# Making the weights' low part with an adding DMA instead of a VectorE subtraction

## The chip, the cores and the metric

The kernel runs on one core of a Trainium2 chip. The metric is the device time of one execution in microseconds; lower is better. The median of three runs before the change is 1457.76 us (1455.7 to 1457.97).

## What is computed

Two layers of a streaming encoder over 640 tokens: 512 frames of one new stream and 16 frames of each of eight running streams. A layer is

```python
proj = rms_norm(x, norm1) @ w_in                       # (640, 1024) @ (1024, 1536)
mix  = concat(rg_lru(proj), s5(proj), attention(proj)) # 256 + 256 + 512 columns
x = x + mix @ w_out                                    # (1024, 1024)
act = square(relu(rms_norm(x, norm2) @ w_up))          # (1024, 4096)
x = x + act @ w_down                                   # (4096, 1024)
```

with one more RMSNorm at the end. Everything is float32, and most of the arithmetic is in the four weight matrices of each layer.

## The kernel before

**Layout.** The 640 tokens are two groups of 320 (256 frames of the prompt and 64 of the samples), `g` = 0 and 1. Activations stand transposed, channels on the 128 partitions, tokens along the free dimension.

**Split products.** The matmuls take `float32r` operands, and each operand is held as a high part in that type and the rest. A unit of weights is 1024 x 128, loaded as two halves of 128 x 4 x 128 (256 KB): `raw` by SyncE's queue (`wload`, issue at L229 through `dma`). `wunit` (L237 to L246) makes two tiles of each half: `wh` (the high part, ScalarE, L243) and `wl` (the low part, raw minus high, VectorE, L244). `product` (L248 to L255) then runs, for each of eight blocks of 128 rows, three matmuls of 320 columns into one PSUM bank: high by high (L252), high by low of the activations (L253), low by high (L254). A half therefore feeds 12 matmuls for one group of tokens.

**Buffers.** `raw`, `wh` and `wl` each have four buffers, so weights are made up to four halves ahead of their use. A buffer of `raw` comes free when both `wh` and `wl` have been made from it; buffers of `wh` and `wl` when the product has read them.

**Stages.** `in_proj` (12 units per layer and group), the mixers (`lru`, `s5`, `attention`; small matmuls with much work on VectorE, ScalarE and GpSimd), `out_proj` (8 units), and `mlp` in four quarters of 8 units of `w_up` and 8 of `w_down`. The second and third quarter run both groups on each unit (`mlp(L, 1, (0, 1), ...)`), so a half feeds 24 matmuls there; everywhere else it feeds 12. In all 544 halves are loaded and split: 192 + 192 + 96 + 64 of w_up, w_down, w_in and w_out. `out_proj` and the last quarter also run the next norm's parts for each finished tile: L268 and L281 on ScalarE, L269 on VectorE, L288 on GpSimd.

**Order.** The program is written stage by stage; a scheduler that simulates time fixes the order of the instructions on each engine, and places the work of one stage's mixers between the products of others. Every engine then takes its own list in order. GpSimd's list before holds no DMA.

Of the kernel before, what the change touches and what calls it, by code (L numbers as in the profile page):

```python
# [11 lines left out]
F32 = mybir.dt.float32  # L12
F32R = mybir.dt.float32r
I32 = mybir.dt.int32
AF = mybir.ActivationFunctionType
# [35 lines left out]
def _cols(a):  # L51
    """(..., 128 r) vectors as columns."""
    a = np.asarray(a)
    return a.reshape(-1, 128).T
# [5 lines left out]
def _layout(inputs):  # L60
    """The arrays in the order in which the chip reads them: moves of elements only."""
# [6 lines left out]
    def tiles(w):  # L68
        # (1024, 128 n) -> (n, 128 p, 8 k, 128)
        return w.reshape(8, 128, -1, 128).transpose(2, 1, 0, 3)  # L70
# [9 lines left out]
    # small vectors, one column each  # L80
# [13 lines left out]
    # S5 input and output matrices: halves (re, im) and (im, re) on the partitions  # L94
# [53 lines left out]
def encoder_kernel(ctx: ExitStack, tc: tile.TileContext, a, o):  # L148
# [35 lines left out]
    # ------------------------------------------------------------ constants  # L184
# [4 lines left out]
    # the table of the exponentials comes in before the first load has landed  # L189
# [41 lines left out]
    # ------------------------------------------------------------ weights  # L231
# [5 lines left out]
    def wunit(src, raws=None):  # L237
        out = []
        for n in range(2):
            raw = raws[n] if raws else wload(src, n)  # L240
            h = wp.tile([128, 4, 128], F32R, tag="wh", name="wh")
            l = wp.tile([128, 4, 128], F32R, tag="wl", name="wl", bufs=4)
            act(h, raw, AF.Copy)  # L243
            tt(l, raw, h.bitcast(F32), OP.subtract)  # L244
            out.append((h, l))
        return out  # L246
# [10 lines left out]
    # ------------------------------------------------------------ norms  # L257
    class Norm:
# [41 lines left out]
        def rsqrt(self):  # L300
            """8/3 / sqrt(mean + eps) with the tokens on the partitions (0-127, 128-255, 192-319)."""
# [5 lines left out]
            # a first guess from the exponent, one step of second order and one of third  # L307
# [23 lines left out]
    # ------------------------------------------------------------ small vectors  # L331
# [6 lines left out]
    # ------------------------------------------------------------ accurate exp on small tiles  # L338
    def exp_small(out, x, n):
        """out = exp(x) on [128, n], to about one unit in the last place."""  # L340
# [16 lines left out]
    # ------------------------------------------------------------ LRU constants  # L357
# [24 lines left out]
    # ------------------------------------------------------------ S5 constants  # L382
# [49 lines left out]
    def cmul(eng, out, jout, wr, wis, z, jz, tmp, conj=False):  # L432
        """out = w z (stacked halves), jout = its halves swapped; wis has the half's sign."""
        A, B = (OP.subtract, OP.add) if conj else (OP.add, OP.subtract)
        eng.tensor_tensor(tmp, wis, jz, OP.mult)
        eng.tensor_tensor(out, wr, z, OP.mult)
        eng.tensor_tensor(out, out, tmp, A)
        if jout is not None:
            eng.tensor_tensor(tmp, wis, z, OP.mult)
            eng.tensor_tensor(jout, wr, jz, OP.mult)  # L440
            eng.tensor_tensor(jout, jout, tmp, B)

    def s5_const(L):
# [10 lines left out]
        # input matrices: slot s of a pair of groups is abar^(3-s) Bbar  # L454
# [15 lines left out]
        # output matrices  # L470
# [9 lines left out]
        # causal products inside a block: those with the block's last output, then the rows moved up  # L480
# [9 lines left out]
        # rotation tables by doubling  # L490
# [37 lines left out]
    # ------------------------------------------------------------ per layer small tensors  # L528
# [12 lines left out]
    # ------------------------------------------------------------ input projection  # L541
    def gelu2(eng, out, x):
        """out = 2 gelu(x)"""
# [97 lines left out]
    # ------------------------------------------------------------ RG-LRU  # L641
    def lru(L, P, g, q, mix, c):
# [10 lines left out]
        for ct in range(2):  # L653
# [4 lines left out]
            # the newest rows before the convolution  # L658
# [7 lines left out]
            # decay a = exp(-2 w) and 1 - a^2 = tanh(w) (1 + a)^2  # L666
# [7 lines left out]
        # injection of the running states into the column before each sample  # L674
# [18 lines left out]
    # ------------------------------------------------------------ S5  # L693
    def s5(L, P, g, q, mix, c):
        K = P["S5"]
        u = q.ub
        # zz takes the place of U
# [5 lines left out]
        # inputs by blocks: rows (group of the pair, t, channel)  # L703
# [41 lines left out]
        # outputs  # L745
# [18 lines left out]
        # states after the last block  # L764
# [22 lines left out]
    # ------------------------------------------------------------ attention  # L787
    def attention(L, P, g, q, mix, c):
        # the samples' scratch
        kcT, p = c.at(0, 2, 2, 144), [c.at(640 + 288 * n, 2, 144) for n in range(2)]  # L790
        vc, pt = c.at(1280, 2, 2, 128), [c.at(640 + 288 * n, 2, 128) for n in range(2)]
        # those of the second pair of samples start at partition 32
        half = [slice(32 * n, 32 * n + 16) for n in range(2)]
        vn, pn = ([c.at(o, 2, 128)[h] for h in half] for o in (1792, 2048))
        # the prompt's, in the same place: keys' windows of 192 columns with 64 zeros on each side
# [18 lines left out]
        def soft(b, x, sk, nsk, one):  # L814
            """Exponentials of the scores in b over their sum with the sink's."""
# [116 lines left out]
    # ------------------------------------------------------------ output projection and MLP  # L932
# [39 lines left out]
    # ------------------------------------------------------------ the program  # L972
# [14 lines left out]
    # the tensor engine's clock rises while the first loads are under way  # L987
# [31 lines left out]
    # ------------------------------------------------------------ final norm  # L1019
# [36 lines left out]
```

## Time and profile before

| what | value |
|---|---|
| runs | 1455.7, 1457.76, 1457.97 us (median 1457.76) |
| profiled execution, from its first to its last instruction | 1454.2 us |
| median of the runs over that span | 3.6 us more |
| TensorE, matmuls | 1404.7 us busy, 97% |
| VectorE | 924.5 us, 64% |
| ScalarE | 662.4 us, 46% |
| GpSimd | 377.0 us, 26% |
| DMA from HBM | 151.02 MB read, mean of all traffic 107 GB/s |
| mean granted TensorE clock | 0.979 of 2.4 GHz |

A group of instructions is one line of the kernel on one engine; "idle before" is the time that the engine stood still right before such instructions, and what ended it. Matmuls are pipelined, so the 314 ns of one overlap with the next: the step from one to the next is about 0.147 us. Where an engine is not the one that ends a stretch, its idle time costs nothing.

### The profile page before, as it was taken

To read this page: it belongs to the slowest core of one execution; us is meant where nothing else is said; L and a number is where in the kernel's file an instruction comes from. 1 tells how busy PE (TensorE), PEld (TensorE's weight loads), DVE (VectorE), ACT (ScalarE), POOL (GpSimd) and SP (SyncE) were. 2 spreads that over 40 slices of the span, in tenths; PEclk is the share of its full clock that TensorE was granted. 3 is DMA by queue.
4 is the path that set the end of the run, shared out by engine and by line. 5 is a ranking of instruction groups with operands and counts; after the bars stand their busy time and mean duration, and the time that the engine had idled before them with its cause. 6 is when DMAs were issued, how large, how long until landed. Compare 5 with 4: busy or idle time off the path is not lost.

```text
span 1454.2 us, 25829 instructions
## 1 busy us (share of the span) xinstructions
PE 1404.7 (97%) x9540; PEld 1336.3 (92%) x9540; DVE 924.5 (64%) x1858; ACT 662.4 (46%) x1387; POOL 377.0 (26%) x565
## 2 busy tenths in 40 slices
PE   7699999999999999999999999999999999999997
PEld 7688688899999999999987898789999999999997
DVE  8999889856544344357687768875664434434564
ACT  6566565545422122135674667453543312313543
POOL 3847269401010011072244225320110100100111
PEclk9999899999999999999998999899999999999998
DMA  6232122344422222234422342224443222223452
GB/s 244 86 109 81 50 95 97 105 150 140 152 80 78 76 80 73 73 107 157 140 91 73 120 137 92 68 95 145 149 146 106 73 73 73 80 78 104 153 174 94
DMA packets 91389, 156.27 MB, mean 107 GB/s; under 512 B 14336, under 2 KB 18304, under 8 KB 91264
## 3 DMA queue, kind: packets, MB, share of 16 engines
q1 hardware_dynamic: 91264, 154.63, 32.0%
q8 instruction: 75, 1.23, 0.4%
q14 instruction: 50, 0.41, 0.1%
HBM read 151.02 MB, written 3.37 MB: 106 GB/s over the span
## 4 chain that ended last, share of the span: by engine, by line
PE 80%; DVE 11%; POOL 4%; issue 3%; ACT 2%; DMA 1%; SPq 0%; DVEq 0%; POOLq 0%
PE mm L254 24%; PE mm L252 24%; PE mm L253 24%; DVE wl L244 2%; PE att L899 1%; PE att L878 1%; PE s L755 1%; PE s L753 1%; PE att L176 1%; PE s L176 1%; PE fin L326 0%; PE att L663 0%; PE s L721 0%; PE s L779 0%; DVE bigr L269 0%
## 5 line engine op out<-in xcount | busy, mean ns | idle before, releaser
L254 PE MATMUL mm<-bigr,wl 128*128 128x320 f32 x2688 | 840.9, 314 | 22.6 <-DVE wl L244 22.6
L252 PE MATMUL mm<-bigr,wh 128*128 128x320 f32 x2688 | 840.2, 313 | 1.7 <-ACT wh L243 1.1
L253 PE MATMUL mm<-bigr,wh 128*128 128x320 f32 x2688 | 839.1, 313 | 1.0 <-DVE bigr L269 1.0
L243 ACT ACTIVATE wh<-raw 128x512 fp32r<-128x512 f32 x544 | 340.7, 630 | 494.4 <-PE mm L253 469.9
L254 PEld LDWEIGHTS mm<-bigr,wl 128*128 128x128 f32 x2688 | 509.8, 190 | 34.7 <-DVE wl L244 27.4
L252 PEld LDWEIGHTS mm<-bigr,wh 128*128 128x128 f32 x2688 | 509.4, 190 | 7.9 <-issue 5.0
L253 PEld LDWEIGHTS mm<-bigr,wh 128*128 128x128 f32 x2688 | 509.5, 190 | 6.9 <-issue 3.9
L244 DVE TENSOR_TENSOR wl<-raw,wh 128x512 fp32r<-128x512 f32 x544 | 399.7, 736 | 179.6 <-ACT wh L243 158.9
L156 POOL TENSOR_SCALAR bigr<-t 128x320 fp32r<-128x320 f32 x128 | 63.0, 493 | 566.3 <-ACT t L952 566.3
L934 DVE TENSOR_TENSOR xT<-xT,mm 128x320 f32<-128x320 f32 x160 | 77.7, 486 | 127.5 <-PE mm L254 127.4
L952 ACT ACTIVATE t<-t 128x320 f32<-128x320 f32 x128 | 59.9, 470 | 137.9 <-DVE t L951 132.3
L954 DVE TENSOR_TENSOR bigr<-t,bigr 128x320 fp32r<-128x320 f32 x128 | 69.7, 546 | 69.6 <-POOL bigr L156 69.3
L951 DVE SCALAR_TENSOR_TENSOR t<-mm,r 128x320 f32<-128x320 f32 x124 | 60.6, 488 | 81.5 <-PE mm L254 81.4
L288 POOL TENSOR_TENSOR ss<-ss,sq 128x320 f32<-128x320 f32 x58 | 56.9, 981 | 195.7 <-ACT sq L281 185.6
L833 POOL TENSOR_SCALAR att<-att,st 128x192 f32<-128x192 f32 (+3 forms) x40 | 37.2, 931 | 79.5 <-DVE st L831 43.6
L824 ACT ACTIVATE att<-att,st 128x192 f32<-128x192 f32 (+3 forms) x80 | 30.7, 389 | 28.3 <-DVE st L822 22.1
L269 DVE SCALAR_TENSOR_TENSOR bigr<-xT,sm,bigr 128x320 fp32r<-128x320 f32 x64 | 39.7, 629 | 3.8 <-ACT bigr L268 3.6
L268 ACT ACTIVATE bigr<-xT,sm 128x320 fp32r<-128x320 f32 x64 | 34.4, 558 | 11.1 <-DVE xT L934 7.8
L281 ACT ACTIVATE sq<-xT 128x320 f32<-128x320 f32 x66 | 30.4, 460 | 9.9 <-DVE xT L934 3.7
L878 PE MATMUL att<-kT,q 64*64 64x192 f32 (+2 forms) x256 | 28.1, 329 | 2.5 <-ACT att L824 2.1
L605 POOL TENSOR_TENSOR sw<-sw,cs 128x320 f32<-128x320 f32 x20 | 19.4, 969 | 33.6 <-ACT sw L604 28.3
L176 PE MATMUL att<-ident,att 128*128 128x128 f32 (+1 forms) x144 | 24.6, 280 | 3.2 <-DVE att L833 1.0
(287 smaller groups left out, 1078.6 us busy)
## 6 DMA issues: line engine op xcount, KB each, us to landing
raw<-w_up SPq DMA_DIRECT2D x192, 256.0 KB, 2.6
raw<-w_down SPq DMA_DIRECT2D x192, 256.0 KB, 2.6
raw<-w_in SPq DMA_DIRECT2D x96, 256.0 KB, 2.6
raw<-w_out SPq DMA_DIRECT2D x64, 256.0 KB, 2.5
xT<-x SPq DMA_DIRECT2D x8, 320.0 KB, 5.7
yT<-xT SPq DMA_DIRECT2D x8, 320.0 KB, 2.5
cs<-rope SPq DMA_DIRECT2D x4, 320.0 KB, 4.4
gg<-gg SPq DMA_DIRECT2D x2, 512.0 KB, 5.1
```

The lines of the kernel that those rows point to most:

```text
L156: return G.tensor_scalar(out, in_, 1.0, 0.0, OP.mult, OP.add)
L176: PE.transpose(out, in_, ident[0:n, 0:n])
L243: act(h, raw, AF.Copy)
L244: tt(l, raw, h.bitcast(F32), OP.subtract)
L252: mm(pt, lhsT=h[:, k % 4], rhs=m[:, k, 0], start=k == 0, stop=False)
L253: mm(pt, lhsT=h[:, k % 4], rhs=m[:, k, 1], start=False, stop=False)
L254: mm(pt, lhsT=l[:, k % 4], rhs=m[:, k, 0], start=False, stop=k == 7)
L288: G.tensor_tensor(self.ss, self.ss, sq, OP.add)
L934: tt(xT[:, g, k], xT[:, g, k], pt, OP.add)
L951: V.scalar_tensor_tensor(t, pt, 0.0, norm.r, OP.max, OP.mult)
L952: act(t, t, AF.Square)
L954: tt(am[:, f, 1], t, am[:, f, 0].bitcast(F32), OP.subtract)
```

## The change

The low part is no longer raw minus high on VectorE. ScalarE writes the negative of the high part into `wl`, and a DMA issued from GpSimd's queue adds `raw` to it in place (`wl += raw`). The high part, the loads, the matmuls and the number of buffers stay. The diff's other lines delete comments and texts; they do nothing. After L244 all line numbers are one higher.

```diff
@@ -241,7 +241,8 @@
             h = wp.tile([128, 4, 128], F32R, tag="wh", name="wh")
             l = wp.tile([128, 4, 128], F32R, tag="wl", name="wl", bufs=4)
             act(h, raw, AF.Copy)
-            tt(l, raw, h.bitcast(F32), OP.subtract)
+            act(l, h.bitcast(F32), AF.Copy, scale=-1.0)
+            G.dma_start(l, raw, accum_op=OP.add)
             out.append((h, l))
         return out
```

A buffer of `raw` now comes free when the adding DMA has landed, and so does `wl` become ready.

The scheduler places the new instructions. ScalarE's list in the first output projection (`out_proj`, layer 0, group 0) before the change; `wh` from `raw` is a high part, `bigr` and `sq` are the next norm's parts (L268, L281):

```order
L243 ACTIVATE wh_3748<-raw_3746 128x512
L243 ACTIVATE wh_3754<-raw_3752 128x512
L268 ACTIVATE bigr_3574<-xT_85,sm_86 128x320
L281 ACTIVATE sq_3700<-xT_85 128x320
L243 ACTIVATE wh_3791<-raw_3789 128x512
L243 ACTIVATE wh_3797<-raw_3795 128x512
L268 ACTIVATE bigr_3574<-xT_85,sm_86 128x320
L281 ACTIVATE sq_3743<-xT_85 128x320
```

The same place after the change (L269 and L282 are the former L268 and L281, L244 is the negative of the high part):

```order
L243 ACTIVATE wh_3814<-raw_3812 128x512
L269 ACTIVATE bigr_3670<-xT_85,sm_86 128x320
L282 ACTIVATE sq_3757<-xT_85 128x320
L244 ACTIVATE wl_3815<-wh_3814 128x512
L243 ACTIVATE wh_3852<-raw_3850 128x512
L244 ACTIVATE wl_3853<-wh_3852 128x512
L243 ACTIVATE wh_3859<-raw_3857 128x512
L269 ACTIVATE bigr_3670<-xT_85,sm_86 128x320
L282 ACTIVATE sq_3802<-xT_85 128x320
L244 ACTIVATE wl_3860<-wh_3859 128x512
```

Of the two halves of a unit, one has the norm's two instructions between its high part and its low part now; the other has them next to each other.

GpSimd's list at that place before the change holds the norm's running sums (`ss`, L288) alone:

```order
L288 TENSOR_TENSOR ss_3575<-ss_3575,sq_3657 128x320
L288 TENSOR_TENSOR ss_3575<-ss_3575,sq_3700 128x320
L288 TENSOR_TENSOR ss_3575<-ss_3575,sq_3743 128x320
L288 TENSOR_TENSOR ss_3575<-ss_3575,sq_3786 128x320
L288 TENSOR_TENSOR ss_3575<-ss_3575,sq_3829 128x320
```

After the change it holds two adds (L245) for each sum (now L289), and parts of the S5 tables (`tab`), which the scheduler has moved here from an earlier place:

```order
L245 DMA wl_3815<-raw_3812 128x512
L518 TENSOR_TENSOR tab_93<-tab_93 128x16x31
L245 DMA wl_3853<-raw_3850 128x512
L506 TENSOR_TENSOR tab_93<-tab_93 128x16
L289 TENSOR_TENSOR ss_3671<-ss_3671,sq_3802 128x320
L245 DMA wl_3860<-raw_3857 128x512
L514 TENSOR_TENSOR tab_93<-tab_93 128x16x31
L515 TENSOR_TENSOR tab_93<-tab_93 128x16x31
L517 TENSOR_TENSOR tab_93<-tab_93 128x16x31
L245 DMA wl_3898<-raw_3895 128x512
```

An add stands behind whatever GpSimd has in front of it, the sum of the last tile among that.

## Rows read from the trace of the kernel before

**Rows 1.** The page: busy time, and the span in 40 slices.
```profile
PE 1404.7 (97%) x9540; PEld 1336.3 (92%) x9540; DVE 924.5 (64%) x1858; ACT 662.4 (46%) x1387; POOL 377.0 (26%) x565
PE   7699999999999999999999999999999999999997
```

**Rows 2.** The page: the chain that ended last, shares of the span by engine and line.
```profile
PE 80%; DVE 11%; POOL 4%; issue 3%; ACT 2%; DMA 1%; SPq 0%; DVEq 0%; POOLq 0%
PE mm L254 24%; PE mm L252 24%; PE mm L253 24%; DVE wl L244 2%; PE att L899 1%; PE att L878 1%; PE s L755 1%; PE s L753 1%; PE att L176 1%; PE s L176 1%; PE fin L326 0%; PE att L663 0%; PE s L721 0%; PE s L779 0%; DVE bigr L269 0%
```

**Rows 3.** Groups by line: busy us, mean ns | idle us before, what ended it.
```profile
L254 PE MATMUL mm<-bigr,wl 128*128 128x320 f32 x2688 | 840.9, 314 | 22.6 <-DVE wl L244 22.6
...
L244 DVE TENSOR_TENSOR wl<-raw,wh 128x512 fp32r<-128x512 f32 x544 | 399.7, 736 | 179.6 <-ACT wh L243 158.9 <-PE mm L253 11.9
L243 ACT ACTIVATE wh<-raw 128x512 fp32r<-128x512 f32 x544 | 340.7, 630 | 494.4 <-PE mm L253 469.9 <-DMA raw<-w_in 8.3 <-PE mm L254 3.9
...
L288 POOL TENSOR_TENSOR ss<-ss,sq 128x320 f32<-128x320 f32 x58 | 56.9, 981 | 195.7 <-ACT sq L281 185.6 <-DVE rsq L310 6.6 <-ACT st L829 3.4
...
L268 ACT ACTIVATE bigr<-xT,sm 128x320 fp32r<-128x320 f32 x64 | 34.4, 558 | 11.1 <-DVE xT L934 7.8 <-DMA xT<-x 2.4
...
L281 ACT ACTIVATE sq<-xT 128x320 f32<-128x320 f32 x66 | 30.4, 460 | 9.9 <-DVE xT L934 3.7 <-POOL ss L288 2.7 <-DVE ss L285 2.2
...
L743 POOL TENSOR_TENSOR bigf<-bigf,tab 128x640 f32<-128x640 f32 x8 | 17.7, 2217 | 5.2 <-ACT bigf L741 5.2
```

**Rows 4.** Stretches, L243 alone: length, ScalarE busy (halves), clock, DMA share, GB/s.
```profile
290.80:399.90 109.10, 37.19 (x59) 1.00 0.45 147
399.90:618.00 218.10, 39.23 (x62) 1.00 0.23 77
618.00:654.40 36.40, 9.95 (x17) 1.00 0.35 107
654.40:727.10 72.70, 24.16 (x40) 1.00 0.45 148
...
836.20:872.50 36.30, 11.12 (x18) 1.00 0.43 137
...
981.60:1090.60 109.00, 38.46 (x61) 1.00 0.44 147
...
1127.00:1308.80 181.80, 32.92 (x52) 1.00 0.23 76
1308.80:1345.10 36.30, 10.06 (x16) 1.00 0.30 104
1345.10:1417.80 72.70, 24.73 (x40) 1.00 0.49 164
```

**Rows 5.** Timelines in the first full-rate stretch: start us, length us, engine, line, what.
```profile
301.56 0.63 ACT L243 ACTIVATE wh<-raw 128x512 fp32r<-128x512 f32 x1 [1.13 <-PE mm L253]
303.32 0.63 ACT L243 ACTIVATE wh<-raw 128x512 fp32r<-128x512 f32 x1 [1.13 <-PE mm L253]
...
302.22 0.69 DVE L244 TENSOR_TENSOR wl<-raw,wh 128x512 fp32r<-128x512 f32 x1 [1.07 <-ACT wh L243]
...
302.94 0.33 SPq L229 DMA_DIRECT2D raw<-w_out  x1
```

**Rows 6.** DMA issues: count, KB each, us to landing; last, raw's landings, 290.8:399.9.
```profile
raw<-w_up SPq DMA_DIRECT2D x192, 256.0 KB, 2.6
...
raw<-w_out SPq DMA_DIRECT2D x64, 256.0 KB, 2.5
...
tab<-bc SPq DMA_DIRECT2D x4, 256.0 KB, 4.5
...
Mm<-Mm SPq DMA_DIRECT2D x4, 24.0 KB, 1.9
...
DMA to landing us min/median/max: 2.5/2.6/3.7
```

**Rows 7.** Two stretches: length, busy us (instructions) of PE, PEld, DVE, ACT, POOL.
```profile
0.00:290.80 290.80, 259.17 (x1724) 224.30 (x1725) 263.36 (x614) 175.73 (x424) 172.41 (x236) 0.95 0.33 108
290.80:399.90 109.10, 109.10 (x741) 107.43 (x740) 64.51 (x116) 50.00 (x88) 9.29 (x14) 1.00 0.45 147
```

**Rows 8.** Chain that ended last, by line: within 0:290.8, then within 727.1:981.6.
```profile
by line: issue 8.6%; DVE wl L244 8.0%; PE mm L254 7.2%; PE mm L252 6.7%; PE mm L253 6.7%; PE s L755 3.1%; PE att L878 3.0%; PE s L753 2.8%; PE att L899 2.5%; PE s L721 2.0%; DVE bigf L657 2.0%; PE att L176 1.8%; DVE bigr L269 1.8%; DMA xT<-
...
by line: PE mm L252 16.6%; PE mm L253 16.4%; PE mm L254 16.2%; issue 4.5%; PE att L878 4.2%; PE att L899 4.0%; DVE wl L244 3.4%; PE s L755 2.6%; PE att L176 2.5%; PE s L753 2.3%; POOL bigf L743 1.9%; PE s L779 1.8%; PE s L176 1.4%; PE att L
```

## The prediction

> **What bounds the kernel now.** I read the page first. TensorE is busy 97% of the span of 1454.2 us, in nearly every slice, VectorE 64%, ScalarE 46%, GpSimd 26% [rows 1]. The chain that ended last says the same: 80% is TensorE, with 72% on lines 252 to 254, the three matmuls of a product; VectorE holds 11%, and the line that this change removes, L244, 2% [rows 2]. The groups show how little TensorE waits for it: 22.6 us in all before the low parts' matmuls, released by L244 [rows 3]. So what can be won is some 20 to 30 us, although 544 instructions of 736 ns (399.7 us) leave VectorE. The question is whether the new way of making a low part is as well hidden as the old one.
>
> For that I cut the span into stretches by how fast weight halves (128x512, one instruction of L243 each) are used [rows 4]. Five stretches run at full rate, 59 + 40 + 18 + 61 + 40 = 218 halves in 109.1 + 72.7 + 36.3 + 109.0 + 72.7 = 399.8 us, 1.83 us each, with the DMA engines busy 0.43 to 0.49. Two stretches (62 and 52 halves, 399.9 us) use each half for both token groups and need one only every 3.5 us. The rest (the first 290.8 us, the mixers of layer 1, changes of stage) uses one in 2 to 3.3 us.
>
> The timeline inside the first full-rate stretch shows the ring [rows 5]. ScalarE writes a high part of 0.63 us every 1.76 us, each time released by L253, that is when TensorE has finished with the buffer of four halves before. VectorE's low part follows 0.03 us later, and 0.03 us after that ends SyncE issues the next load, because the raw buffer is free. A load lands 2.6 us after its issue (at most 3.7 here) [rows 6]. Four buffers make a lap 4 x 1.76 = 7.04 us. Used of it today: 0.63 + 0.03 + 0.69 + 0.03 + 2.6 = 3.98 us. The raw ring has 3.06 us to spare. That spare time is what the change spends.
>
> **The change, part by part.**
>
> *Removed:* L244 on VectorE. In the full-rate stretches VectorE is not the limit (64.5 of 109.1 us busy [rows 7]), so there it gives nothing. In the first 290.8 us VectorE is busy 263.4 us [rows 7] and L244 has 8.0% of the chain, 23 us; in 727 to 982 us 3.4%, 9 us [rows 8]. Upper bound of the gain: 32 us.
>
> *Added on ScalarE:* 544 copies, written as the high part is (128x512, 630 ns [rows 3]): 343 us, of which none is new waiting where ScalarE has room: 50.0 + 59 x 0.63 = 87 of 109.1 us in the first full-rate stretch [rows 7, 4]. One place is tight. During an output projection each product (two halves, 3.52 us) also has L268 and L281, 558 + 460 ns [rows 3]; with 4 x 0.63 that is 3.54 us. There the new order puts those two between a high part and its low part, which adds 1.02 us to every second lap. 64 halves are of that kind (w_out [rows 6]), up to 1.02 / 4 = 0.26 us each: 16 us.
>
> *Added on GpSimd:* 544 issues. The trace has no DMA from this queue. The nearest rows are SyncE's issue of 0.33 us [rows 5] from below, and from above GpSimd's long instructions, 0.98 us (L288) to 2.2 us (L743) [rows 3]. I take 1.0 us, since an engine that has to work a descriptor list out is nearer to a long instruction than to SyncE's. In the full-rate stretches GpSimd is nearly idle (9.3 of 109.1 us) and 59 us more fit. In the first 290.8 us its 172.4 us [rows 7] grow by 88 to 260, so that the bound of that stretch moves from VectorE to GpSimd rather than goes away. I set the two against each other at zero there, with ends of -32 us and +40 us (every other one of 88 issues holding up something for its 1.0 us).
>
> *Added on the DMA engines, and the wait:* a low part is now ready when an add of 256 KB, SBUF to SBUF, has landed. Call A the time from ScalarE's copy to that landing. Two things wait for A: TensorE, and the raw buffer, which the add still reads, so SyncE's next load is behind it. TensorE needs the low part three halves after the high part was begun, 5.28 us plus 0.1 us; the copies take 1.32 us, so A may be 4.1 us. The raw lap is 0.63 + 0.03 + 0.63 + 0.03 + A + 0.03 + 2.6 = 3.95 + A, so there A may be only 3.1 us. The raw ring gives way first.
>
> A from rows: a small copy within SBUF takes 1.9 us from issue to landing, a 256 KB load 2.6 [rows 6], so 256 KB of transfer are 0.7 us. An add has three streams (raw in, low part in, low part out) where a load has two: 1.5 times, 1.05 us. GpSimd's issue is 0.65 us longer than SyncE's. A = 1.9 + 1.05 + 0.65 = 3.6 us, and a lap of 7.55 us gives 1.89 us per half. Bounds: 2.6 us if the add goes like a load from SyncE, and 7 us if issue and transfer behave like the slowest landings of a transfer this size (4.5 us, tab<-bc [rows 6]) with 2.2 us of GpSimd before it.
>
> The 16 DMA engines are a second limit. A half costs them 0.45 x 109.1 / 59 = 0.83 us now [rows 4]. With an add of 1.25 us at 1.5 times it is 2.08 us, above the 1.76 us that TensorE needs. Loads and adds then stand behind one another, half of the other's transfer on average, 0.9 us per lap: (7.55 + 0.9) / 4 = 2.11 us. Both limits say a little over 2.1. I take 2.15 us, since 1.5 is the least that three streams can mean.
>
> *Sum.* Full-rate stretches: 218 x 2.15 - 399.8 = +69 us. Output projections: +16. First stretch and mixers: 0. Stretches at 3.5 us per half: 0, as 2.15 is far below. That makes 1454.2 + 85 = 1539.2 us of span. The median of the runs, 1457.76 us, stands 3.6 us above the profiled span: 1543 us.
>
> **The rivals.**
>
> *Two full reads.* If the read side of the DMA engines is the limit, an add costs twice a load, 0.83 + 1.66 = 2.49 us per half: 218 x 2.49 - 399.8 = +143 us, and about 1601 us. For it: a load's 0.7 us for 256 KB is already near all that the engines do. Against it: no row separates read and write. The Trainium skill (Collectives: The Full Stack, section "The bandwidth ceiling: the fold count and why AG ≠ RS ≠ AR") holds that an add in the DMA path runs at half a copy's rate because it reads two sources; no run here shows it yet, and by it this rival would be the forecast. Chance 0.2.
>
> *Adds much slower still, or GpSimd the gate.* With A = 7 us a half takes (3.95 + 7) / 4 = 2.74 us: 218 x 2.74 - 399.8 = +198, and some +18 where 17 and 16 halves fall into 36 us [rows 4]: about 1673 us. GpSimd works in order, so an add behind an instruction that waits for a mixer gives the same picture. Against it: GpSimd is idle nine tenths of the full-rate stretches. Chance 0.15.
>
> *The ring holds, and VectorE's relief is all that is left.* The point is A = 3.1 us. With the add at 2.6 to 3.1 us from copy to landing and the DMA engines not in each other's way, the full-rate stretches stay at 1.76 us, and of the 32 us on the chain half come back: about 1442 us, faster. For it: 0.5 us is all that separates my 3.6 from it. Against it: the DMA engines would have to do 2.08 us of work in 1.76. Chance 0.11, of which 0.04 that gain and new waits cancel.
>
> *A little over:* A of 3.2 to 3.5 us and little queueing, 1461 to 1500 us, chance 0.1. The forecast itself, 1500 to 1575 us, has the rest, 0.44.
>
> **How the numbers follow.** A measurement of this kernel can tell about 0.2%, 3 us, from no change. Faster 0.07, same 0.04, all other cases slower, 0.89. Below 1465 us lies 0.11, and above 1690 us, past the third case, some 0.08; the range is 1465 to 1690 us.
>
> **What the profile after would show.** Right: VectorE's busy time near 525 us, ScalarE's near 1005; in the full-rate stretches high parts every 2.0 to 2.3 us, with ScalarE's L243 released by the load of raw where it now is by L253; TensorE's idle time before lines 252 and 254; DMA share near or above 0.8 there; adds landing 3.5 to 4.5 us after issue; the 3.5 us stretches as long as before. Wrong: high parts still every 1.76 us (the ring held); or lines 254 waiting for GpSimd's queue with raw long landed (GpSimd is the gate); or the 3.5 us stretches longer, which needs A above 10 us.

## The result

The change makes the kernel slower: 1706.36 us (median of four runs, 1695.44 to 1709.08) against 1457.26 us, a ratio of 1.170 [1.166, 1.174]. The forecast was 1543 us with a range to 1690 us: the direction was right, the loss of 249 us is nearly three times the 85 us that were worked out.

The page of the profile after (a span of 1702.2 us), which answers to [rows 1]: busy time, TensorE's 40 slices, and the two DMA queues (packets, MB, share of the 16 engines' time).

```profile
span 1702.2 us, 27064 instructions
PE 1481.5 (87%) x9540; PEld 1369.2 (80%) x9540; DVE 565.2 (33%) x1314; ACT 966.6 (57%) x1931; POOL 802.0 (47%) x1109
PE   6779989768789999978899888987878999997786
q0 software_dynamic: 78336, 142.64, 48.2%
q1 hardware_dynamic: 91264, 154.63, 28.1%
```

TensorE's row of nines has holes in it now. The second queue, q0, is new: it holds the adds, 142.64 MB (544 of 256 KB), and they take more of the DMA engines than the kernel's whole other traffic on q1. The chain that ended last, to be laid beside [rows 2], shows what filled the holes:

```profile
PE 42%; DMA 31%; ACT 10%; DVE 7%; issue 6%; POOL 2%; SPq 0%; ACTq 0%; POOLq 0%; DVEq 0%
DMA wl<-raw 13%; PE mm L255 13%; PE mm L253 12%; PE mm L254 12%; DMA raw<-w_down 7%; DMA raw<-w_up 5%; ACT wh L243 4%; DMA raw<-w_in 3%; ACT wl L244 3%; DMA raw<-w_out 3%; POOL wl L245 1%; DMA tab<-bc 1%; PE att L879 1%; PE att L900 1%; DVE bigf L740 1%
```

TensorE's share fell from 80% to 42%, and DMA's rose from 1% to 31%: 13% are the adds, wl<-raw, and some 18% the loads of raw. The groups (busy us, mean ns | idle us before, what ended it), beside [rows 3]; L253 to L255 are the former L252 to L254:

```profile
L255 PE MATMUL mm<-bigr,wl 128*128 128x320 f32 x2688 | 868.4, 326 | 132.1 <-DMA wl<-raw 131.4
L253 PE MATMUL mm<-bigr,wh 128*128 128x320 f32 x2688 | 858.0, 320 | 48.5 <-ACT wh L243 46.0 <-issue 2.0 <-DVE t L609 0.2
...
L245 POOL DMA_DIRECT2D wl<-raw x544 | 495.0, 927 | 681.4 <-ACT wl L244 628.3 <-issue 11.5 <-DMA raw<-w_down 9.3
L243 ACT ACTIVATE wh<-raw 128x512 fp32r<-128x512 f32 x544 | 341.4, 628 | 541.8 <-PE mm L254 220.0 <-DMA raw<-w_down 121.6 <-DMA raw<-w_up 97.1
L244 ACT ACTIVATE wl<-wh 128x512 fp32r<-128x512 f32 x544 | 340.7, 628 | 12.6
```

TensorE stands 132.1 us before low parts that have not landed (22.6 us before), and 48.5 us before high parts. L243 used to be released almost by TensorE alone; now some 220 us of its idle time end with a load of raw. That is the raw ring: the load comes late because the add has held its buffer. SyncE's own waits (us in total, times, longest) show it, in the changed kernel and before:

```profile
SPq L229 <- DMA wl<-raw: 1367.6, 524, 11.1
```

```profile
SPq L229 <- DVE wl L244: 965.7, 464, 10.0
```

GpSimd's issue is 0.93 us, and 628 of the 681 us before it end with ScalarE's copy.

**Where the 248 us lie.** Cut by stages (from the first low-part matmul of a stage to that of the next, in both traces), the spans differ as follows:

```
                                         halves   before us   after us   difference
until the first low-part matmul                       7.9       15.7       +7.8
in-projections to up-projection, layer 0   80       272.2      301.3      +29.1
full rate, one group                      224       422.0      597.5     +175.5
both groups on a half, 3.5 us             128       452.2      450.3       -1.9
mixers of layer 1 and what lies in them   112       300.0      337.5      +37.5
```

The full-rate stages went from 1.88 to 2.67 us per half. Windows of four pieces (length, busy us of PE, PEld, DVE, ACT and POOL, granted clock, DMA share, GB/s): the start, a 3.5-us stretch, layer 1's second in-projection, and one full-rate stage of 16 halves.

```profile
0.00:113.50 113.50, 79.34 (x427) 72.79 (x428) 74.94 (x241) 75.08 (x154) 68.93 (x115) 0.80 0.70 175
491.50:716.50 225.00, 225.00 (x1535) 225.00 (x1536) 46.67 (x96) 93.30 (x159) 69.74 (x96) 1.00 0.65 152
968.40:1046.00 77.60, 65.47 (x432) 58.44 (x431) 34.98 (x71) 60.62 (x122) 46.58 (x65) 0.96 0.80 180
1134.00:1175.10 41.10, 31.09 (x192) 28.34 (x193) 4.80 (x10) 20.08 (x34) 15.62 (x19) 1.00 0.92 202
```

In the full-rate stage TensorE is busy for 31.1 of 41.1 us and every other computing engine for half of it or less, the granted clock is 1.00, its upper level, and the DMA engines are 0.92 busy (0.43 to 0.49 before [rows 4]). In the 3.5-us stretch TensorE has no hole, with the same adds under it.

One lap of the ring in that full-rate stage, first from the timeline of ScalarE (start us, length us; in brackets the idle time before, and what ended it):

```profile
1142.05 0.64 ACT L243 ACTIVATE wh<-raw 128x512 fp32r<-128x512 f32 x1 [3.76 <-PE mm L253]
1142.72 0.63 ACT L244 ACTIVATE wl<-wh 128x512 fp32r<-128x512 f32 x1
1144.19 0.63 ACT L243 ACTIVATE wh<-raw 128x512 fp32r<-128x512 f32 x1 [0.84 <-DMA raw<-w_down]
```

then from that of GpSimd:

```profile
1143.65 0.86 POOL L245 DMA_DIRECT2D wl<-raw  x1 [4.17 <-ACT wl L244]
```

The landings in that stage, of the adds (by the tile wl) and of the loads (by their line, L229):

```profile
DMA to landing us min/median/max: 3.5/4.6/6.2
...
DMA to landing us min/median/max: 2.8/3.6/5.1
```

and those of the adds in a 3.5-us stretch, 1468 to 1524 us:

```profile
DMA to landing us min/median/max: 3.2/3.3/3.8
```

ScalarE's copy ends at 1143.35 and GpSimd issues 0.3 us later. Followed through the trace, from one high part to the next one made from the same buffer, the laps that begin in that stage take, in the mean, 0.63 + 0.03 + 0.63 + 0.29 us to the add's issue, 4.75 to its landing, 0.08 to the load's issue, 3.61 to its landing, and 0.25 until ScalarE takes it up: 10.27 us, a fourth of it 2.57 us. The stage took 41.1 / 16 = 2.57. The chain within it agrees, with 79% of it in these two kinds of transfer:

```profile
by line: DMA raw<-w_down 37.2%; DMA wl<-raw 33.1%; issue 10.9%; DMA raw<-w_out 8.8%; ACT wh L243 4.7%; ACT wl L244 4.5%; POOL wl L245 1.3%; ACT t L953 1.1%; POOLq L245 0.2%; SPq L229 0.2%; ACTq L243 0.1%
```

So the ring closes at 2.57 us. But its transfers are slow because they share the engines: where nothing presses, an add lands in 3.3 us, and a load took 2.6 us before [rows 6]. Theory 1 says that the DMA engines are the limit: an add of 0.482 x 1702.2 / 544 = 1.51 us of all 16 and a load of 0.281 x 1702.2 / 544 x 142.6 / 154.6 = 0.81 us (the weights are 142.6 of q1's 154.63 MB) make 2.3 us per half, whatever the buffers. That price is not made by the crowding itself: the 3.5-us stretch above, where TensorE never waits, has 0.65 x 225.0 / 64 = 2.29 us for each of its 64 halves. Theory 2, the rival, says that the four raw buffers are: with more of them the loss would go.

### The profile page after: what moved, and what is told of

Read it like the earlier page. It is cut to its first block, busy times and chain, and to the rows that moved or that the text cites. A ratio compares the mean times of both kernels' runs of the same rounds, so it can differ in the third digit from the quotient of the medians.

```text
span 1702.2 us, 27064 instructions
## 1 busy us (share of the span) xinstructions
PE 1481.5 (87%) x9540; PEld 1369.2 (80%) x9540; DVE 565.2 (33%) x1314; ACT 966.6 (57%) x1931; POOL 802.0 (47%) x1109
## 3 DMA queue, kind: packets, MB, share of 16 engines
q0 software_dynamic: 78336, 142.64, 48.2%
q1 hardware_dynamic: 91264, 154.63, 28.1%
## 4 chain that ended last, share of the span: by engine, by line
PE 42%; DMA 31%; ACT 10%; DVE 7%; issue 6%; POOL 2%; SPq 0%; ACTq 0%; POOLq 0%; DVEq 0%
DMA wl<-raw 13%; PE mm L255 13%; PE mm L253 12%; PE mm L254 12%; DMA raw<-w_down 7%; DMA raw<-w_up 5%; ACT wh L243 4%; DMA raw<-w_in 3%; ACT wl L244 3%; DMA raw<-w_out 3%; POOL wl L245 1%; DMA tab<-bc 1%; PE att L879 1%; PE att L900 1%; DVE bigf L740 1%
## 5 line engine op out<-in xcount | busy, mean ns | idle before, releaser
L255 PE MATMUL mm<-bigr,wl 128*128 128x320 f32 x2688 | 868.4, 326 | 132.1 <-DMA wl<-raw 131.4
L253 PE MATMUL mm<-bigr,wh 128*128 128x320 f32 x2688 | 858.0, 320 | 48.5 <-ACT wh L243 46.0
L254 PE MATMUL mm<-bigr,wh 128*128 128x320 f32 x2688 | 850.0, 317 | 0.0
L245 POOL DMA_DIRECT2D wl<-raw x544 | 495.0, 927 | 681.4 <-ACT wl L244 628.3
L255 PEld LDWEIGHTS mm<-bigr,wl 128*128 128x128 f32 x2688 | 519.5, 194 | 180.7 <-DMA wl<-raw 170.8
L243 ACT ACTIVATE wh<-raw 128x512 fp32r<-128x512 f32 x544 | 341.4, 628 | 541.8 <-PE mm L254 220.0
L253 PEld LDWEIGHTS mm<-bigr,wh 128*128 128x128 f32 x2688 | 521.9, 194 | 64.5 <-ACT wh L243 57.0
L254 PEld LDWEIGHTS mm<-bigr,wh 128*128 128x128 f32 x2688 | 521.9, 194 | 3.9 <-issue 3.3
L244 ACT ACTIVATE wl<-wh 128x512 fp32r<-128x512 f32 x544 | 340.7, 628 | 12.6
L955 DVE TENSOR_TENSOR bigr<-t,bigr 128x320 fp32r<-128x320 f32 x128 | 65.6, 515 | 259.3 <-POOL bigr L156 259.3
L156 POOL TENSOR_SCALAR bigr<-t 128x320 fp32r<-128x320 f32 x128 | 87.2, 684 | 75.9 <-ACT t L953 72.9
L289 POOL TENSOR_TENSOR ss<-ss,sq 128x320 f32<-128x320 f32 x58 | 61.1, 1054 | 40.1 <-ACT sq L282 40.0
L270 DVE SCALAR_TENSOR_TENSOR bigr<-xT,sm,bigr 128x320 fp32r<-128x320 f32 x64 | 44.1, 696 | 72.0 <-ACT bigr L269 72.0
L269 ACT ACTIVATE bigr<-xT,sm 128x320 fp32r<-128x320 f32 x64 | 34.3, 549 | 7.3 <-DVE xT L935 4.7
L282 ACT ACTIVATE sq<-xT 128x320 f32<-128x320 f32 x66 | 30.1, 457 | 7.9 <-DVE ss L286 4.1
```

Source lines behind the costliest of these rows:

```text
L156: return G.tensor_scalar(out, in_, 1.0, 0.0, OP.mult, OP.add)
L244: act(l, h.bitcast(F32), AF.Copy, scale=-1.0)
L245: G.dma_start(l, raw, accum_op=OP.add)
L253: mm(pt, lhsT=h[:, k % 4], rhs=m[:, k, 0], start=k == 0, stop=False)
L254: mm(pt, lhsT=h[:, k % 4], rhs=m[:, k, 1], start=False, stop=False)
L255: mm(pt, lhsT=l[:, k % 4], rhs=m[:, k, 0], start=False, stop=k == 7)
```

## The experiments

All changes below are against the changed kernel. The last table of this section has their stages side by side.

### Is it the added work on ScalarE?

The DMA goes, ScalarE's negative copy stays, and VectorE adds raw to it.

```diff
-            G.dma_start(l, raw, accum_op=OP.add)
+            tt(l, raw, l.bitcast(F32), OP.add)
```

> ScalarE writes the negative of the high part as in the change, and VectorE adds raw to it: no DMA from GpSimd. This is ScalarE's part of the change alone. Theories 1 and 2: ScalarE has room nearly everywhere, 1455 to 1475 us. Theory 4 (ScalarE's second copy and its place in ScalarE's order cost a good part of the 249 us): 1500 us or more.

Measured: 1459.2 us, ratio 1.0015 [0.9997, 1.0033]. ScalarE has all its 544 more instructions here:

```profile
PE 1404.4 (96%) x9540; PEld 1337.1 (92%) x9540; DVE 906.3 (62%) x1858; ACT 965.1 (66%) x1931; POOL 386.3 (27%) x565
```

With ScalarE at the 965 us of the changed kernel nothing is lost that can be told from no change. So the cost lies with the DMA, its issue and its transfer, and with what waits for them.

### Ring or engines?

**Seven raw buffers** in place of four (other buffers shrink to make room: `ub`, `q`, `qS` from two to one).

```diff
-        raw = wp.tile([128, 4, 128], F32, tag="raw", name="raw", bufs=4)
+        raw = wp.tile([128, 4, 128], F32, tag="raw", name="raw", bufs=7)
```

> The change with seven buffers of raw in place of four; to make room, ub, q and qS have one buffer in place of two, which can hold up the mixers, but not the products of the two feed-forward halves. Theory 1 (the DMA engines are the limit: an add takes them as long as two loads, about 1.5 us beside 0.75 us of a load): a half of a weight unit still takes 2.25 to 2.35 us where one token group uses it, instead of 2.6 us, and the time falls by about 75 us, to 1630 us, DMA share there 0.95 or more. Theory 2 (waiting is the limit: the landing of the add holds one of four raw buffers, nothing is saturated): raw no longer binds, a half takes 1.76 to 1.95 us, and the time is 1500 to 1540 us.

Measured: 1603.95 us, ratio 1.100 [1.092, 1.108], between the 1630 us of theory 1 and the 1500 to 1540 of theory 2. Its queues, and the window of a full-rate stage of 16 halves:

```profile
q0 software_dynamic: 78336, 142.64, 51.0%
q1 hardware_dynamic: 91264, 154.63, 30.6%
```

```profile
1178.70:1214.70 36.00, 32.39 (x195) 28.57 (x195) 4.49 (x10) 20.44 (x34) 14.49 (x18) 1.00 1.03 233
```

36.0 / 16 = 2.25 us per half with the DMA share at 1.03 (it adds up the packets' times, and so can pass 1): the engines are full. Adds landed in 5.5 us at the median there and loads in 4.7, later than with four buffers, with (5.5 + 4.7) / 2.25 = 4.5 transfers under way at once in place of (4.75 + 3.61) / 2.57 = 3.3. The raw ring no longer closes: seven buffers and a lap of 0.63 + 0.03 + 0.63 + 0.3 + 5.5 + 0.05 + 4.7 = 11.84 us would allow 1.69 us, and in that stage the high parts wait for TensorE again:

```profile
L243 ACT ACTIVATE wh<-raw 128x512 fp32r<-128x512 f32 x17 | 10.7, 631 | 15.8 <-PE mm L254 15.7
```

TensorE gives back a buffer of `wh` here, of which there are still four. In the four stages from 1073.3 to 1214.7 us the lap of that second ring, from one high part to the next in the same buffer, is 9.1 us in the mean, 5.4 of them the add's landing, and a fourth is 2.27 us. So three more raw buffers took 0.35 to 0.4 us per half away, and what is left stands at the 2.2 to 2.3 us of theory 1, with full engines, whose late landings reach TensorE through the second ring. No run gave `wh` and `wl` more buffers; that the engines alone would hold 2.3 us is worked out, not measured.

**Adds for every second half only** (the other halves are subtracted on VectorE).

```diff
+            if n == 1:
                 act(l, h.bitcast(F32), AF.Copy, scale=-1.0)
                 G.dma_start(l, raw, accum_op=OP.add)
+            else:
+                tt(l, raw, h.bitcast(F32), OP.subtract)
```

> The first half of each unit by VectorE as before, the second by the adding DMA: 272 adds. Theory 1 alone (engines): a half costs the engines 0.75 + 0.75 = 1.5 us on average, less than 1.76, so the full-rate stages are back at 1.76 us and the time at 1455 to 1490 us. Theory 2 (the landing in the raw ring): the buffers that the adds hold still need 0.63 + 0.03 + 0.63 + 0.3 + 3.2 to 3.6 + 0.03 + 2.6 to 3.0, that is 7.4 to 8.2 us a lap and 1.86 to 2.05 us per half: 1490 to 1540 us.

Measured: 1524.3 us, ratio 1.046 [1.037, 1.054]. The engines need 0.81 + 0.75 = 1.6 us per half now, below TensorE's 1.76, and yet 2.13 us pass (1.86 to 2.05 were expected of theory 2). A late add holds one raw buffer of two, and the ring waits for it all the same: theory 2 at work without theory 1.

### What makes the add dear?

**A plain copy** in place of the add; the subtraction is left out.

```diff
-            G.dma_start(l, raw, accum_op=OP.add)
+            G.dma_start(l.bitcast(F32), raw)
```

> The change with a plain copy of raw into the low part's tile in place of the add, from the same queue, with the same waits; the subtraction is left out. Theory 1 (the add's second read fills the DMA engines): a 2 KB packet of this queue takes about 84 ns where the add's took 178, a half costs the engines 1.5 us, less than TensorE's 1.76, and the time comes down to 1460 to 1490 us. Theory 2 (four raw buffers and the landing): the landing falls by 0.75 us from 3.2 us undisturbed, a lap of 6.7 us, also under 7.04: 1460 to 1490 us. Theory 3 (GpSimd's issue and its order are the limit, 0.87 us each): nothing changes for GpSimd, a half stays at 2.4 us or more and the time above 1650 us.

Measured: 1576.8 us, ratio 1.082 [1.065, 1.098], so that about half of the loss stays, far more than expected. The copy costs the engines 0.236 x 1565 / 544 = 0.68 us; with the load's 0.81 that is below 1.76, and the share in a full-rate stage is only 0.71. What holds it is mostly the ring again: copies and loads land in 3.4 us there, the lap is 0.63 + 0.03 + 0.63 + 0.3 + 3.4 + 0.03 + 3.4 = 8.4 us, or 2.1 us per half. The stages show 2.04 and 2.13.

The expectation had counted with undisturbed landings. Two things differ between this copy and the add, though, since the copy is declared float32 at both ends and moves in fewer and larger packets. Two more runs part them: a copy whose destination is float32r as the add's is (the subtraction is left out again), and the add with a float32 destination.

```diff
-            G.dma_start(l, raw, accum_op=OP.add)
+            G.dma_start(l, raw)
```

```diff
-            G.dma_start(l, raw, accum_op=OP.add)
+            G.dma_start(l.bitcast(F32), raw, accum_op=OP.add)
```

> The changed kernel with a copy in place of the add (the subtraction is left out), its destination declared float32r as the add's is; the earlier copy was declared float32 on both sides, took 0.68 us of the 16 DMA engines per half in packets of 4 KB, and gave 1577 us. Theory R, the add is dear because it reads two sources: this copy is as cheap as the float32 one, 0.65 to 0.8 us per half, 1560 to 1590 us. Theory T, it is dear because of the destination's type (or its 2 KB packets): 1.4 to 1.5 us per half on the engines, 1690 to 1715 us.

> The changed kernel's add, unchanged but for its destination, declared float32 on both sides. Theory R: still about 1.5 us of the engines per half, 1690 to 1715 us. Theory T: about 0.7 us, and 1560 to 1590 us.

Measured: 1587.34 us, ratio 1.090 [1.087, 1.094], and 1707.73 us, ratio 1.172 [1.162, 1.182]. Queue and issue of the float32 copy:

```profile
q0 software_dynamic: 43520, 142.64, 23.6%
...
L245 POOL DMA_DIRECT2D wl<-raw x544 | 303.5, 558 | 685.8 <-ACT wl L244 635.4
```

the same of the float32r copy, whose span is 1586.8 us:

```profile
q0 software_dynamic: 78336, 142.64, 28.7%
...
L245 POOL DMA_DIRECT2D wl<-raw x544 | 301.8, 555 | 704.0 <-ACT wl L244 646.8
```

and of the float32 add, whose span is 1694.3 us:

```profile
q0 software_dynamic: 78336, 142.64, 48.6%
...
L245 POOL DMA_DIRECT2D wl<-raw x544 | 496.4, 926 | 671.8 <-ACT wl L244 626.4
```

The float32r copy has the add's packet count and costs 0.287 x 1586.8 / 544 = 0.84 us of the engines; the add costs 1.51 us with either type. The destination's type explains 0.16 us, the adding 0.67 us. At equal packets an add is 1.8 times a copy. The Trainium skill (Collectives: The Full Stack, section "The bandwidth ceiling: the fold count and why AG ≠ RS ≠ AR") says of the adds of a ReduceScatter that they run at half a copy's rate because they read two sources; the accumulating DMA of these runs, 1.8 times a copy, agrees to within a tenth. The runs do not show the reading itself. The add also takes GpSimd 0.93 us to issue where a copy takes 0.56.

**Both at once: seven buffers and the plain copy** (the subtraction is left out; the two edits above together).

> Both reliefs at once: seven raw buffers (ub, q, qS with one buffer) and the plain copy in place of the add; the subtraction is left out. If the two causes, the add's second read and the landing in the raw ring, are all that lengthens the full-rate stages, a half takes 1.76 to 1.9 us there (2.22 us with the buffers alone, 2.0 to 2.3 with the copy alone) and the time is 1490 to 1530 us, what is left being made in the input projections. If GpSimd's issue or its order has a share of its own, a half stays at 2.0 us or more and the time above 1550 us.

Measured: 1524.07 us, ratio 1.045 [1.040, 1.049]. The full-rate stages take 2.04 us per half; the time lies in the first range of the expectation, the pace in the second. That completes a square of four runs, loss in the 224 full-rate halves against the kernel before:

```
                    add       copy
4 raw buffers      +176        +75
7 raw buffers       +91        +36
```

Three more buffers save 85 us with adds and 39 us with copies; the copy in place of the add saves 101 us and 55 us. The trace shows what holds the last 36 us: in the three stages from 1064.4 to 1158.8 us the high parts wait for TensorE alone,

```profile
L243 ACT ACTIVATE wh<-raw 128x512 fp32r<-128x512 f32 x49 | 30.8, 630 | 24.0 <-PE mm L254 23.9
```

and the lap of the second ring, that of `wh`, is 8.2 us in the mean, 3.9 of them the copy's landing: a fourth is 2.06 us. No run with more buffers of `wh` and `wl` tried it.

### The in-projections

Even there the four in-projections stayed as long as in the changed kernel, 336 us together against 334. They had been forecast at no cost. So the adds were put **into the in-projections alone** (96 of 544 halves; `add` is true in `in_proj`, all others subtract on VectorE).

```diff
+            if add:
                 act(l, h.bitcast(F32), AF.Copy, scale=-1.0)
                 G.dma_start(l, raw, accum_op=OP.add)
+            else:
+                tt(l, raw, h.bitcast(F32), OP.subtract)
```

> Adds for the 96 halves of the input projections alone; all other low parts by VectorE as before. In the change the stretches with mixers lost 67 us beside 175 us in the full-rate stages. If that loss is made by the adds of the input projections themselves: 1505 to 1535 us, with the stages in0 and in1 20 to 30 us longer each. If it is only mixers' work that the scheduler has moved from the output projections into them: 1455 to 1480 us.

Measured: 1505.82 us, ratio 1.032 [1.027, 1.037]: 47 us from 96 adds, 0.5 us each, while the feed-forward stages are as before the change. Two runs take the reasons apart: the same 96 as plain copies from GpSimd's queue, and as plain copies from ScalarE's own queue (both leave the subtraction of these halves out).

```diff
-                G.dma_start(l, raw, accum_op=OP.add)
+                G.dma_start(l.bitcast(F32), raw)
```

```diff
-                G.dma_start(l, raw, accum_op=OP.add)
+                nc.scalar.dma_start(l.bitcast(F32), raw)
```

> As the run with adds in the input projections alone (1505.8 us), but each of its 96 adds is a plain copy from GpSimd's queue (the subtraction is left out there). Theory A, the input projections lose time to the add's price on the DMA engines: the copy moves in 0.68 us of the engines instead of 1.5, so most of the +47 us goes, 1465 to 1480 us. Theory B, they lose it to the order of things: the high part, its copy and the issue stand in the in-order lists of ScalarE and GpSimd between the mixers' work, and any transfer there is as late: 1490 to 1506 us.

> The same 96 plain copies, issued from ScalarE's own queue right behind its copy, so that GpSimd's list is out of it (the subtraction is left out here too). If GpSimd's list is what makes them late (theory B, GpSimd), 1465 to 1480 us; if it is ScalarE's list, or the landing as such, within 8 us of the run with copies from GpSimd's queue.

Measured: 1483.45 us, ratio 1.018 [1.014, 1.022], and 1465.43 us, ratio 1.005 [1.003, 1.007]. Issue and landing (last number, us) of these transfers, in the order adds, copies from GpSimd, copies from ScalarE:

```profile
wl<-raw POOLq DMA_DIRECT2D x96, 256.0 KB, 4.4
```

```profile
wl<-raw POOLq DMA_DIRECT2D x96, 256.0 KB, 3.0
```

```profile
wl<-raw ACTq DMA_DIRECT2D x96, 256.0 KB, 2.7
```

The 47 us fall apart into some 22 for the add's price, some 18 for going by GpSimd instead of ScalarE's queue, and 7 for the rest. The 18 are not one effect. In the start and the mixers of layer 0 ScalarE's queue is 25 us ahead, in layer 1's mixers 9 us behind (the last table of the experiments), and each of these programs was scheduled anew. ScalarE's copies land 0.3 us sooner than GpSimd's; an issue starts 0.83 us after ScalarE has written the negative where GpSimd does it, and 0.54 us where ScalarE does, in the mean; and GpSimd's issues take its time, 0.56 us each in the run with copies everywhere. These were not parted. Neither theory A nor theory B held alone: A expected 1465 to 1480, B 1490 or more, and the run lies between them. The run with ScalarE's queue lies in the range that was given for GpSimd's list as the cause (1465 to 1480), but by the points above the list alone is not shown to be it. The stages of the in-projections themselves lose more than the total, and stages behind them win some back (in layer 1 the output projection of group 0 is 14 us shorter with the adds), as mixers' work is done while TensorE waits. GpSimd's list has the mixers' work between the adds there. In the run with 96 adds (span 1502.3 us) 31 of them were issued more than 0.5 us after ScalarE's negative was written. The longest such wait, first ScalarE's list, then GpSimd's:

```profile
44.74 0.62 ACT L245 ACTIVATE wl<-wh 128x512 fp32r<-128x512 f32 x1
```

```profile
54.57 0.12 POOL L497 MEMSET tab<- 128x16 f32 x1 [4.83 <-DVE tab L441]
54.64 0.72 POOL L445 TENSOR_TENSOR tab<-tab 128x256 f32<-128x256 f32 x1
55.33 0.86 POOL L574 TENSOR_TENSOR ub<-ub,r 128x320 f32<-128x320 f32 x1
56.13 0.89 POOL L246 DMA_DIRECT2D wl<-raw  x1
```

The negative is there at 45.36 us. GpSimd has other work before the add, stands still for 4.83 us of that time until VectorE has a piece of the S5 tables ready, and issues the add at 56.13, 10.8 us late. At another place the add is not late by GpSimd at all:

```profile
898.32 0.87 POOL L246 DMA_DIRECT2D wl<-raw  x1 [1.30 <-ACT wl L245]
901.55 0.88 POOL L609 TENSOR_TENSOR sw<-sw,cs 128x320 f32<-128x320 f32 x1 [2.36 <-ACT sw L608]
906.08 0.89 POOL L246 DMA_DIRECT2D wl<-raw  x1 [3.65 <-ACT wl L245]
```

Here GpSimd waits 2.36 us for ScalarE to hand it a piece of a finished projection, and 3.65 us for ScalarE's negative, which itself stood behind the next high part, and that behind a load.

### Can the new way be used where VectorE is the busier?

VectorE is the busiest engine of the first stretch (263.4 of 290.8 us [rows 7]), so the low parts of group 0's output projections (32 halves, both layers, beside the mixers' end) were tried with the add (the branch is that of the last section), and, as an alternative, with GpSimd subtracting; everything else on VectorE.

```diff
-            w = wunit(a["w_out"][L, k])
+            w = wunit(a["w_out"][L, k], add=g == 0)
```

For the second, the branch taken where `g == 0` is

```diff
+                G.tensor_tensor(l, raw, h.bitcast(F32), OP.subtract)
```

> Adds for the 32 halves of the first token group's output projections alone, where VectorE has the mixers to do and a half is used in 3.8 to 4.5 us; all other low parts by VectorE. If a slow half hides the landing and VectorE's relief counts, 1440 to 1455 us; if the relief is not on the path or GpSimd's order eats it, 1457 to 1465 us.

> The kernel before, with the subtraction of the same 32 halves on GpSimd instead of VectorE, without any DMA. It relieves VectorE by the same 32 instructions. If VectorE's relief in the output projections is worth anything, 1440 to 1455 us; if GpSimd is as much on the path there (an instruction of this size takes it 1.5 us or more), 1457 to 1475 us.

Measured: 1459.72 us, ratio 1.0015 [0.9992, 1.0039], and 1459.52 us, ratio 1.0003 [0.9982, 1.0025]. Neither gains. In the first the output projection of layer 0 grew by 15 us and later stages gave it back. No version tried beats the kernel before.

The stages of all runs against the kernel before, in us of the profiled execution (columns as in the table of the result; the last is the time per half in the 224 full-rate halves, 1.88 before):

```
                              start  layer-0 mixers  full rate  both groups  layer-1 mixers   per half
the change                      +8        +29          +176         -2            +38           2.67
seven raw buffers               +9        +36           +91         -2             +9           2.29
adds for every second half       0        +12           +55         -1             +8           2.13
float32 copy                    +7        +17           +75         -2            +14           2.22
float32r copy                   +7        +21           +88         -2            +18           2.28
add, float32 destination        +8        +28          +171         -1            +34           2.65
float32 copy, seven buffers     +6        +25           +36         -2             +3           2.04
adds in in-projections only     +9        +26            -5          0            +18           1.86
  copies from GpSimd there      +7        +21            -2          0             -2           1.88
  copies from ScalarE there     +8         -5            -1          0             +7           1.88
ScalarE negates, VectorE adds   +1         +5            -1         -2             -2           1.88
adds in group 0's out_proj       0        +12            -6          0             -1           1.86
GpSimd subtracts there           0         +6            -6          0             +2           1.86
```

## Why the prediction was right in direction and too small

**Right.** The raw ring is the first to give way: L243 is released by loads of raw, and the run with seven buffers got 102 us back. The lap was built of the right pieces. A without pressure came out as forecast, 0.3 + 3.3 = 3.6 us, but partly by luck: by the forecast's terms a plain copy would take 1.9 + 0.7 + 0.65 = 3.25 us, and one lands 2.3 us after its issue in a 3.5-us stretch of the run with float32 copies, so 0.3 + 2.3 = 2.6 us. What any transfer takes before its data was put too high and the add's extra over a copy too low (1.0 us, not 0.35), and the two cancel. GpSimd's issue, taken at 1.0 us, measured 0.93. The 3.5-us stretches stayed as long as they were. VectorE's relief brought nothing that could be kept: 565 us busy in place of 924, and a slower kernel.

**The step that failed first** is the add's price on the DMA engines, taken as three streams where a load has two: 1.25 us of the 16 engines, and 2.08 us per half with the load. Measured are 1.51 us and, with the load, 2.2 to 2.3. The rival "Two full reads" had the better price for the add (1.66 us); its 2.49 us per half is about as far above the 2.29 us that seven buffers show as the forecast's 2.08 is below.

**The step that failed second** is how the two limits combine. The forecast put 0.9 us of queueing on a lap of 7.55 us and found both limits near 2.1. With the engines 0.92 busy, an add took 1.45 us more than undisturbed and a load 1.0 us more (4.75 and 3.61 us in the mean against 3.3 and 2.6), 2.45 us per lap and not 0.9; another 0.25 us went by until ScalarE took the load up. So the limits do not stand side by side, with the larger one deciding. Engines that are nearly full lengthen both landings, and the ring turns that into a pace above either: the run with seven buffers stands near the engines' limit with 2.29 us per half, and four buffers make it 2.67, not 2.15. The rival "Adds much slower still" had the pace nearly (2.74 us) from another make-up: all of it in an A of 7 us, where A was 0.3 + 4.75 = 5.05 us and the load took its share. The full-rate stages lost 176 us where 69 and, for the output projections, 16 were forecast; these two steps are 90 of the missing 163 us.

**The third** is the zero for "first stretch and mixers". It weighed VectorE's relief against GpSimd's issues, but only by busy time, and left the wait for the add out. Layer 1's two in-projections had used a half in 1.92 and 2.05 us before, faster than the forecast's own 2.15, so that the ring had to slow them as well. The in-projections alone lost 29.3, 4.1, 25.3 and 28.5 us in the order of the program, and the start 7.8 us; with what came back in neighbouring stages it was 74 us, the rest of the missing. The forecast's upper end for this term was 40 us. As the runs with 96 transfers show, about half of such a loss is the add's price and two fifths the way by GpSimd. A part that the forecast did not have at all is the clock: in the first in-projection the granted clock was 1.00 before and 0.80 after, and of the 29.3 us that the stage grew by, TensorE stood idle for 7.3 and was busy for 22.0 (50.94 before, 72.95 after), with slower products and with mixers' matmuls that the schedule has put there. How much of it is the clock was not separated.

**The term of the output projections** (16 us, for the norm's two instructions between a high part and its low part) was half right. At full rate these stages took 46.2 and 44.5 us where the ones right before them took 43.1 and 41.1: 0.19 and 0.21 us per half, against 0.26 forecast, for 32 halves. For the other 32, beside the mixers, there is no such loss. And it is a cost of a ring without slack: with ScalarE's copies there too but no add by DMA (ScalarE negates, VectorE adds), the output projections at full rate take 28.9 and 28.2 us, 28.2 each before.

**The signs to look for.** High parts come every 2.4 to 2.9 us (forecast 2.0 to 2.3), adds land in 4.6 us in a full-rate stage (3.5 to 4.5), the DMA share is 0.92 (near or above 0.8), ScalarE's busy time is 967 us (1005), VectorE's 565 us (525). The last two are mostly a matter of counting: busy time counts an overlap of two instructions once, and the durations themselves, added up, grew by 337.6 us on ScalarE and fell by 387.5 us on VectorE.

## What to carry to other kernels

An operation that is moved to a DMA is not free because the DMA engines are half idle. Work out what it costs all 16 engines (here 1.5 us for an add of 256 KB, 1.8 times a copy), add what is there already, and compare the sum with the time that the bound engine gives; where it comes near, count with landings that are some 1.4 times as long, as here, not with those of an idle machine. Then look at which buffer the transfer holds: an engine's 0.7 us became 0.3 us of issue and 3.3 to 4.6 us of landing in a ring whose slack was 3.1 us, and the next load stood behind it. More buffers for one tile can uncover the next ring: with seven of raw, the four of `wh` set the pace. And an issue from an engine that works in order is as late as the work ahead of it on that engine's list: one add here was issued 10.8 us late.

## What the runs showed of the hardware that was not expected

- The type that a destination is declared with changed how a copy on GpSimd's queue was cut: 43520 packets with float32, 78336 with float32r, at 0.68 and 0.84 us of the engines per 256 KB. For the add it changed nothing.
- The add's issue kept GpSimd busy for 0.93 us, a copy's for 0.56 us.
- More buffers made each transfer slower and the kernel faster: adds land in 5.5 us with seven raw buffers and in 4.6 us with four.
- In stretches in which TensorE waits often the granted clock was lower: 0.80 in the first 113.5 us, the start and the first in-projection, which before the change took 76.4 us at 1.00, and 0.96 in layer 1's second in-projection, again 1.00 before. Some of the loss there may thus be a slower clock, between its levels of 1.2 and 2.4 GHz; how much was not separated. Those first 76.4 us before the change, and then a full-rate stage of 16 halves after it (columns as in the windows above):

```profile
0.00:76.40 76.40, 56.52 (x341) 51.63 (x342) 70.80 (x202) 47.07 (x98) 44.56 (x67) 1.00 0.47 163
```

```profile
716.50:754.90 38.40, 32.87 (x194) 30.44 (x192) 7.45 (x16) 22.35 (x39) 17.18 (x24) 0.91 0.90 200
```

- At full rate the clock did not set the pace: the stage in the last line had 0.91 and took 2.40 us per half, the one read above had 1.00 and took 2.57.
